# V of the dilated groups evicted at full height and reordered by SBUF transfers, with a new beginning and end of the program

## The chip, the cores and the metric

The kernel runs on one core of a Trainium2 chip. The metric is the device time of one execution in microseconds (us); lower is better. Engines are named as in the profile: PE is TensorE (PEld its weight loads), DVE is VectorE, ACT is ScalarE, POOL is GpSimd, SP is SyncE, which here only issues transfers. SPq, ACTq and so on are the instruction queues of the engines.

## The reference

A decoder trunk of two layers on 512 tokens of 1024 numbers, all fp32. Each layer adds half of a SwiGLU network, then a mixer, then half of a second SwiGLU network; a last norm follows.

```python
for l in range(DEPTH):                       # DEPTH = 2
    x = x + 0.5 * swiglu(rms_norm(x, norm_ffn1[l]), ...)
    x = x + hybrid_mixer(rms_norm(x, norm_mix[l]), ...)
    x = x + 0.5 * swiglu(rms_norm(x, norm_ffn2[l]), ...)
return rms_norm(x, norm_final)

def swiglu(x, w_gate, w_up, w_down):
    return (jax.nn.silu(x @ w_gate) * (x @ w_up)) @ w_down
```

The mixer projects its input once to queries, keys and values of 16 heads of 64 and to two gates. Twelve heads are dilated window attention in three groups of four, with dilations 1, 4 and 16 and partial rotary embedding of queries and keys; a query of a group with dilation d reads the tokens t, t-d, t-2d and so on. The groups are merged by their softmax denominators. Four heads are stick-breaking attention: instead of a softmax, a weight is the product of a sigmoid and of all later (1 - sigmoid), which is computed as an exponential of a running sum. The two results are projected, gated, added and projected again.

## The kernel before

**Layout and products.** Activations lie transposed: eight tiles `x0` to `x7` of 128 features by 512 tokens. A product in fp32 is made of three matmuls (`mm3`, lines 141 to 144): activation and weight are each split into a high and a low part in a rounded format, and hi x hi, lo x hi, hi x lo are added in one PSUM bank. `project` (line 146) does so over the eight feature tiles; so a 128 x 512 result costs 24 matmuls. PSUM has eight banks in four pairs with the tags m, t, o and s.

**Weights.** The class `Weights` (lines 45 to 94) streams all weights once, in order of use. SP issues transfers of 512 KB (`wraw`); ACT casts each quarter of 128x512 to its high part (`whi`, line 76) and DVE subtracts it for the low part (`wlo`, line 77), two quarters ahead of their use. A quarter serves four 128x128 blocks, twelve matmuls of 128x512.

**Norm.** `Norm` (lines 157 to 237): `scale` splits x times the gain into `xh` (ACT, line 179) and `xl` (DVE, line 180); `square` sums the squares; `finish` makes the row factor as `rt` (a column per token tile) and, through a matmul against the identity into a PSUM bank `pb`, as `rb` (a copy by ACT, line 236).

**Beginning.** ACT loads its function table, SP issues the gain, x0, the first two weight quarters and the other x tiles, and then the rest of the weights. The first pair of FFN tiles runs the gate projection `pg` to its end, then the up projection `pu`. ACT alone casts the weights.

**Mixer.** First come the values. With tokens as rows, four token tiles of 512 columns are made twice: half 0 holds the values of group 1 and the stick-breaking heads, half 1 those of the groups with dilation 4 and 16. `split_v` (lines 357 to 361) evicts PSUM to SBUF as a high part (ACT, line 359) and a low part (DVE, line 360). Half 0 is evicted in 8 pieces of 128x256 (tiles `v0`, `vs`). Half 1 goes to one tile `v12` in which the rows are ordered by the residue of the token modulo 4; since the engines write other partitions than they read only in blocks of 32, this takes 16 pieces of 32 rows by 512 columns.

Then `qk_pair` (lines 384 to 417) makes the queries and keys of a pair of heads: with rotary embedding, DVE multiplies (line 393) and shuffles (394), POOL multiplies and adds (395, 396), ACT casts (409 for queries, 413 for keys), DVE subtracts (410, 415), and SP copies the high parts of keys from one half of the partitions to the other (414). `stick` (lines 447 to 483) makes the stick-breaking weights of a head in four tiles of 128 to 512 columns: scores on PE (421, 422, 456), three ACT passes (460 to 462), DVE (463), a running sum on DVE (464), a subtraction on DVE (466), an exponential on ACT (467), which leaves `sw` in one of eight buffers with the tag "pp"; then PE transposes (476) and multiplies with the values (480). The dilated heads have scores, a softmax, transposes and the product with `v12` (620). Gates are further projections, evicted by DVE (493), put between these steps so that PE has work.

**What sets the order.** Each engine executes its own queue in order. Which instruction stands where in it is set by a scheduler that simulates the program when it is built and moves instructions within the limits of dependences and buffers; the order of the source is only its starting point. What it decides for one stretch can change with any edit inside it.

**End.** `finale` (lines 277 to 296) does the last two feature tiles in two halves of 256 tokens: DVE adds to x (288), the norm is finished, and eight products of x and `rb` (line 295; DVE for six of them, POOL for the two of `k == 2`) are written out by four transfers on SP (296).

## Time and profile before

| | |
|---|---|
| median of 3 runs | 2169.5 us (2168.34 to 2170.79) |
| profiled execution, time | 2166.81 us |
| its span in the trace | 2165.0 us |
| PE busy | 2136.6 us, 99% |
| DVE busy | 1209.4 us, 56% |
| ACT busy | 892.7 us, 41% |
| POOL busy | 374.4 us, 17% |
| data moved by transfers | 212.80 MB, mean 98 GB/s |

Busy times are unions of the instructions' spans on one engine; PE's instructions overlap in its pipeline, so their single durations are longer than the distance from one to the next. The trace is of one execution, and all times in the sections below are microseconds from the start of its span. The first mixer's values are made from about 380 to 434 us, its stick-breaking heads from 434 us on; the second layer repeats this about 1071 us later.

### The profile page before, as it was taken

To read this page: it belongs to the slowest core of one execution; us is meant where nothing else is said; L and a number is where in the kernel's file an instruction comes from. 1 tells how busy PE (TensorE), PEld (TensorE's weight loads), DVE (VectorE), ACT (ScalarE), POOL (GpSimd) and SP (SyncE) were. 2 spreads that over 40 slices of the span, in tenths; PEclk is the share of its full clock that TensorE was granted. 3 is DMA by queue.
4 is the path that set the end of the run, shared out by engine and by line. 5 is a ranking of instruction groups with operands and counts; after the bars stand their busy time and mean duration, and the time that the engine had idled before them with its cause. 6 is when DMAs were issued, how large, how long until landed. Compare 5 with 4: busy or idle time off the path is not lost.

```text
span 2165.0 us, 25866 instructions
## 1 busy us (share of the span) xinstructions
PE 2136.6 (99%) x9772; PEld 1764.2 (81%) x9772; DVE 1209.4 (56%) x1896; ACT 892.7 (41%) x1572; POOL 374.4 (17%) x396
## 2 busy tenths in 40 slices
PE   8999999999999999999999999999999999999998
PEld 7888888878887888888888888888788788888887
DVE  7544433589867655443354444336897666444433
ACT  5333323566564433332333333236664544333332
POOL 2222100021412122210022220000223212222100
PEclk9999999999999999999999999999999999999999
DMA  4333333232224233323233333333222233323222
GB/s 153 97 97 98 102 105 125 88 93 87 79 74 129 96 97 98 97 97 98 88 98 97 98 98 107 108 117 94 87 83 78 79 126 98 98 97 97 97 90 86
DMA packets 64621, 212.80 MB, mean 98 GB/s; under 512 B 7408, under 2 KB 9456, under 8 KB 64496
## 3 DMA queue, kind: packets, MB, share of 16 engines
q1 hardware_dynamic: 63920, 210.10, 30.4%
q8 instruction: 76, 1.25, 0.2%
q10 hardware_dynamic: 576, 1.05, 0.2%
q14 instruction: 49, 0.40, 0.1%
HBM read 200.63 MB, written 6.29 MB: 96 GB/s over the span
## 4 chain that ended last, share of the span: by engine, by line
PE 91%; DVE 5%; issue 2%; ACT 1%; POOL 1%; DMA 0%; SPq 0%; DVEq 0%; POOLq 0%; ACTq 0%
PE ps_o L142 14%; PE ps_o L143 14%; PE ps_o L144 14%; PE ps_m L142 9%; PE ps_m L143 9%; PE ps_m L144 9%; PE ps_t L143 5%; PE ps_t L142 5%; PE ps_t L144 5%; DVE wlo L77 1%; DVE sc L464 1%; PE ps_o L620 0%; POOL bn L554 0%; ACT pt L545 0%; PE ps_s L422 0%
## 5 line engine op out<-in xcount | busy, mean ns | idle before, releaser
L77 DVE TENSOR_TENSOR wlo<-wraw,whi 128x512 fp32r<-128x512 f32 x736 | 593.6, 809 | 584.1 <-ACT whi L76 583.5
L76 ACT CAST whi<-wraw 128x512 fp32r<-128x512 f32 x736 | 454.8, 621 | 963.0 <-PE ps_o L143 486.3
L142 PE MATMUL ps_m<-xh,whi 128*128 128x512 f32 x992 | 390.8, 394 | 8.7 <-ACT whi L76 6.1
L143 PE MATMUL ps_m<-xl,whi 128*128 128x512 f32 x992 | 391.3, 394 | 0.0
L144 PE MATMUL ps_m<-xh,wlo 128*128 128x512 f32 x992 | 390.4, 394 | 0.5 <-DVE wlo L77 0.5
L142 PE MATMUL ps_o<-fh,whi 128*128 128x512 f32 (+1 forms) x748 | 285.9, 382 | 0.0
L143 PE MATMUL ps_o<-fl,whi 128*128 128x512 f32 (+1 forms) x748 | 285.8, 382 | 0.0
L144 PE MATMUL ps_o<-fh,wlo 128*128 128x512 f32 (+1 forms) x748 | 285.8, 382 | 0.0
L260 POOL TENSOR_TENSOR fg<-fg,fs 128x512 f32<-128x512 f32 x88 | 116.4, 1325 | 867.0 <-ACT fs L259 867.0
L142 PEld LDWEIGHTS ps_m<-xh,whi 128*128 128x128 f32 x992 | 187.6, 189 | 49.2 <-ACT whi L76 7.0
L144 PEld LDWEIGHTS ps_m<-xh,wlo 128*128 128x128 f32 x992 | 187.6, 189 | 39.4 <-DVE wlo L77 2.0
L143 PEld LDWEIGHTS ps_m<-xl,whi 128*128 128x128 f32 x992 | 187.7, 189 | 37.9 <-DVE xl L180 0.8
L144 PE MATMUL ps_t<-xh,wlo 128*128 128x512 f32 x480 | 187.0, 390 | 0.0
L142 PE MATMUL ps_t<-xh,whi 128*128 128x512 f32 x480 | 187.0, 390 | 0.0
L143 PE MATMUL ps_t<-xl,whi 128*128 128x512 f32 x480 | 187.0, 390 | 0.0
L143 PE MATMUL ps_o<-xl,whi 128*128 128x512 f32 x448 | 174.5, 390 | 0.0
L142 PE MATMUL ps_o<-xh,whi 128*128 128x512 f32 x448 | 174.5, 390 | 0.0
L144 PE MATMUL ps_o<-xh,wlo 128*128 128x512 f32 x448 | 174.5, 390 | 0.0
L142 PEld LDWEIGHTS ps_o<-fh,whi 128*128 128x128 f32 x748 | 140.6, 188 | 30.1
L143 PEld LDWEIGHTS ps_o<-fl,whi 128*128 128x128 f32 x748 | 140.6, 188 | 30.0
L144 PEld LDWEIGHTS ps_o<-fh,wlo 128*128 128x128 f32 x748 | 140.6, 188 | 30.0
L261 POOL TENSOR_TENSOR fg<-fg,rb 128x512 f32<-128x512 f32 x88 | 116.3, 1324 | 6.3
(218 smaller groups left out, 2706.6 us busy)
## 6 DMA issues: line engine op xcount, KB each, us to landing
wraw<-in_w_dram SPq DMA_DIRECT2D x367, 512.0 KB, 3.5
spill<-x SPq DMA_DIRECT2D x16, 256.0 KB, 2.1
kh<-kh SPq DMA_DIRECT2D x32, 128.0 KB, 2.7
x<-spill SPq DMA_DIRECT2D x16, 256.0 KB, 3.5
x<-in_x_dram SPq DMA_DIRECT2D x8, 256.0 KB, 4.7
out_dram<-o SPq DMA_DIRECT2D x8, 256.0 KB, 2.2
wraw<-in_w_dram SPq DMA_DIRECT2D x2, 256.0 KB, 3.5
cr<-in_rope_dram ACTq DMA_DIRECT2D x2, 256.0 KB, 2.8
```

The source lines that it names most:

```text
L76: nc.scalar.copy(hi, src)
L77: nc.vector.tensor_sub(lo, src, hi.bitcast(F32))
L142: nc.tensor.matmul(ps, w[0], v[0], start=start, stop=False, skip_group_check=True)
L143: nc.tensor.matmul(ps, w[0], v[1], start=False, stop=False, skip_group_check=True)
L144: nc.tensor.matmul(ps, w[1], v[0], start=False, stop=stop, skip_group_check=True)
L260: nc.gpsimd.tensor_mul(g, g, s)
L261: nc.gpsimd.tensor_mul(g, g, norm.rb)
L464: nc.vector.tensor_tensor_scan(cv[:, ::-1], av[:, ::-1], ones[:, 0:1].to_broadcast([P, w]), 0.0, ALU.add, ALU.mult)
```

## The change

There are three parts, in one diff.

1. *Values.* Half 0 is evicted in 4 pieces of 128x512 into one tile per token tile (`v0s`). Half 1 is evicted in 8 pieces of 128x256 into tiles `vn`, which take the eight "pp" buffers that the `sw` tiles use later. Then 32 transfers of 32 rows by 512 words (64 KB) per mixer, issued by POOL, put the rows into `v12`.
2. *Beginning.* x0 is the first transfer of SP, the weights come in parts of 256 KB between the x tiles, the gain is issued by ACT. DVE casts the first weight quarter. Seven matmuls on a tile of zeros run into an unused bank. The first FFN pair runs over k with `pg` and `pu` side by side, for which the host packs the first 16 weight blocks in that order, and the squares are moved behind the last cast of x.
3. *End.* DVE's products read the norm factor from PSUM (`pb`) instead of its copy; POOL's two go on reading the copy `rb`.

```diff
@@ -31,6 +31,7 @@
+WARM = 7
@@ -54,17 +55,26 @@
         self.ready = {}
         self.done = 0
         self.chunk = None
+        self.early = []
+
+    def load(self, eng):
+
+        c, part = divmod(len(self.early), CB // QB)
+        if part == 0:
+            self.chunk = self.raw.tile([P, CB * P], F32, name="wraw", tag="wraw")
+        o = part * QB * P
+        eng.dma_start(self.chunk[:, o:o + QB * P], self.w[c, :, o:o + QB * P])
+        self.early.append(self.chunk)
 
     def fill(self, q):
         nc = self.nc
         while self.done <= q and self.done < self.nq:
             c, part = divmod(self.done, CB // QB)
-            if part == 0:
+            if self.done < len(self.early):
+                self.chunk = self.early[self.done]
+            elif part == 0:
                 self.chunk = self.raw.tile([P, CB * P], F32, name="wraw", tag="wraw")
-                step = P if c == 0 else CB * P
-                for o in range(0, CB * P, step * QB):
-                    e = min(o + step * QB, CB * P)
-                    nc.sync.dma_start(self.chunk[:, o:e], self.w[c, :, o:e])
+                nc.sync.dma_start(self.chunk, self.w[c])
             src = self.chunk[:, part * QB * P:(part + 1) * QB * P]
             i = self.done - (self.nq - HELD)
             if i < 0:
@@ -73,7 +83,10 @@
             else:
                 hi = self.hold.tile([P, QB * P], F32R, name="whi", tag=f"xh{i}")
                 lo = self.hold.tile([P, QB * P], F32R, name="wlo", tag=f"xl{i}")
-            nc.scalar.copy(hi, src)
+            if self.done:
+                nc.scalar.copy(hi, src)
+            else:
+                nc.vector.tensor_copy(hi, src)
             nc.vector.tensor_sub(lo, src, hi.bitcast(F32))
             self.ready[self.done] = (hi, lo)
             self.done += 1
@@ -121,17 +134,22 @@
     def bank(tag):
         return psum.tile([P, 512], F32, name="ps_" + tag, tag=tag)
 
+    weights = Weights(nc, rawp, splitp, hpool, win)
+    gain = const.tile([P, gains.shape[1]], F32, name="gain")
+    warm = hpool.tile([P, T], F32R, name="warm", tag=f"xh{KD - 1}")
+    nc.vector.memset(warm.bitcast(F32), 0.0)
+    nc.scalar.dma_start(gain, gains)
     nc.scalar.preload_act_table_set(SIGM)
-    gain = const.tile([P, gains.shape[1]], F32, name="gain")
-    nc.sync.dma_start(gain, gains)
-    weights = Weights(nc, rawp, splitp, hpool, win)
     xs = []
     for k in range(KD):
         t = xpool.tile([P, T], F32, name=f"x{k}", tag=f"x{k}")
         nc.sync.dma_start(t, xin[k])
         xs.append(t)
-        if k == 0:
-            weights.fill(0)
+        if k % 2 == 0:
+            weights.load(nc.sync)
+    ps = bank("o")
+    for i in range(WARM):
+        nc.tensor.matmul(ps, warm[:, 0:P], warm, start=True, stop=True, skip_group_check=True)
 
     ident = const.tile([P, P], F32, name="ident")
     make_identity(nc, ident)
@@ -176,7 +194,7 @@
             if not self.last:
                 hi = hpool.tile([P, T], F32R, name=f"xh{k}", tag=f"xh{k}")
                 lo = hpool.tile([P, T], F32R, name=f"xl{k}", tag=f"xl{k}")
-                nc.scalar.activation(hi, x, AF.Copy, bias=0.0, scale=gk)
+                self.cast = nc.scalar.activation(hi, x, AF.Copy, bias=0.0, scale=gk)
                 nc.vector.scalar_tensor_tensor(lo, x, gk, hi.bitcast(F32), ALU.mult, ALU.subtract)
                 self.h[k] = (hi, lo)
 
@@ -234,7 +252,7 @@
                                  start=True, stop=True, skip_group_check=True)
             rb = npool.tile([P, T], F32, name="rb", tag="rb", bufs=2)
             nc.scalar.copy(rb[:, :n * P], pb[:, :n * P])
-            self.rt, self.rb = rt, rb
+            self.rt, self.rb, self.pb = rt, rb, pb
 
     def ffn(norm, nxt, first):
         with ExitStack() as st:
@@ -246,12 +264,20 @@
             hs = []
             for f in range(NF):
                 pg, pu = [bank(b) for b in ("mt", "mt", "oo")[f % 3]]
-                project(pg, norm.h)
-                project(pu, norm.h)
-                if f == 0:
-                    if first:
+                if first and f == 0:
+
+                    for k in range(KD):
+                        if k + 4 < KD:
+                            norm.scale(k + 4)
+                        for ps in (pg, pu):
+                            mm3(ps, weights.block(), norm.h[k], k == 0, k == KD - 1)
+                    with tc.issue_after(norm.cast.ins):
                         for k in range(KD):
                             norm.square(k)
+                else:
+                    project(pg, norm.h)
+                    project(pu, norm.h)
+                if f == 0:
                     norm.finish_wide(nw, onesr)
                 g = wk.tile([P, T], F32, name="fg", tag="fg")
                 s = wk.tile([P, T], F32, name="fs", tag="fs")
@@ -290,9 +316,9 @@
             nxt.finish(c0 // P, (c0 + HT) // P)
             for k in range(0, KD, 2):
                 o = op.tile([P, 2, HT], F32, name="o", tag="o")
-                eng = nc.gpsimd if k == 2 else nc.vector
+                eng, r = (nc.gpsimd, nxt.rb) if k == 2 else (nc.vector, nxt.pb)
                 for i in range(2):
-                    eng.tensor_mul(o[:, i], xs[k + i][:, c], nxt.rb[:, :HT])
+                    eng.tensor_mul(o[:, i], xs[k + i][:, c], r[:, :HT])
                 nc.sync.dma_start(out[k:k + 2, :, c].rearrange("k p t -> p k t"), o)
 
     def mixer(norm, nxt):
@@ -363,17 +389,19 @@
             if half == 0:
                 v0, vs = [], []
                 for j in range(NT):
-                    sc = norm.rt[:, j:j + 1]
-                    for lst, nm, off in ((v0, "v0", 0), (vs, "vs", 256)):
-                        t = vp.tile([P, 4, 2, HD], F32R, name=f"{nm}_{j}", tag=f"{nm}_{j}")
-                        split_v(t, pv[0][j][:, off:off + 256], sc)
-                        lst.append(t)
+                    t = vp.tile([P, 8, 2, HD], F32R, name=f"v0s_{j}", tag=f"v0s_{j}")
+                    split_v(t, pv[0][j], norm.rt[:, j:j + 1])
+                    v0.append(t[:, 0:4])
+                    vs.append(t[:, 4:8])
             else:
                 v12 = vp.tile([P, 4, 8, 2, HD], F32R, name="v12", tag="v12")
                 for j in range(NT):
-                    for r in range(4):
-                        src = slice(32 * r, 32 * r + 32)
-                        split_v(v12[32 * j:32 * j + 32, r], pv[1][j][src], norm.rt[src, j:j + 1])
+                    for g in range(2):
+                        t = pp.tile([P, 4, 2, HD], F32R, name="vn", tag="pp")
+                        split_v(t, pv[1][j][:, 256 * g:256 * g + 256], norm.rt[:, j:j + 1])
+                        for r in range(4):
+                            nc.gpsimd.dma_start(v12[32 * j:32 * j + 32, r, 4 * g:4 * g + 4].bitcast(F32),
+                                              t[32 * r:32 * r + 32].bitcast(F32))
 
         def to_t(ap):
             return ap.rearrange("p (j m r) -> p j r m", j=NT, m=32, r=4)
@@ -689,10 +717,10 @@
         outer.close()
 
     norm = Norm(0, SIGM)
-    for k in range(KD):
+    for k in range(4):
+        if k % 2 == 0:
+            weights.fill(k // 2)
         norm.scale(k)
-        if k == 3:
-            weights.fill(1)
     mask = const.tile([P, 640], F32, name="mask")
     nc.sync.dma_start(mask, masks)
     mnat, mperm, msb = mask[:, 0:256], mask[:, 256:512], mask[:, 512:640]
@@ -758,10 +786,12 @@
 
     import numpy as np
 
-    def ffn(g, u, dn):
+    def ffn(g, u, dn, first=False):
         g = a[g][l].reshape(KD, P, NF, P).transpose(2, 0, 1, 3)
         u = a[u][l].reshape(KD, P, NF, P).transpose(2, 0, 1, 3)
         gu = np.stack([g, u], 1).reshape(-1, P, P)
+        if l == 0 and first:
+            gu[:2 * KD] = gu[:2 * KD].reshape(2, KD, P, P).transpose(1, 0, 2, 3).reshape(-1, P, P).copy()
         dn = a[dn][l].reshape(NF, P, KD, P).transpose(2, 0, 1, 3).reshape(-1, P, P)
         return [gu, dn]
 
@@ -798,7 +828,7 @@
-    return ffn("ffn1_w_gate", "ffn1_w_up", "ffn1_w_down") + mix + ffn("ffn2_w_gate", "ffn2_w_up", "ffn2_w_down")
+    return ffn("ffn1_w_gate", "ffn1_w_up", "ffn1_w_down", True) + mix + ffn("ffn2_w_gate", "ffn2_w_up", "ffn2_w_down")
```

Some line numbers move: in the new file ACT's weight cast is line 87, the rotary lines on POOL are 423 and 424, the casts of queries and keys 437 and 441, the stick-breaking lines on ACT 488 to 490 and 495.

PE at the very beginning of the program, before; `ps_m` is the gate product, `xh` and `xl` are the parts of x0, x1 and so on.

```order
L142 MATMUL ps_m<-xh_111,whi 128x512
L143 MATMUL ps_m<-xl_112,whi 128x512
L144 MATMUL ps_m<-xh_111,wlo 128x512
L142 MATMUL ps_m<-xh_115,whi 128x512
L143 MATMUL ps_m<-xl_116,whi 128x512
L144 MATMUL ps_m<-xh_115,wlo 128x512
```

The same place after; `ps_t` is the up product.

```order
L152 MATMUL ps_o<-warm 128x512 x7
L160 MATMUL ps_m<-xh_124,whi 128x512
L160 MATMUL ps_t<-xh_124,whi 128x512
L161 MATMUL ps_m<-xl_125,whi 128x512
L161 MATMUL ps_t<-xl_125,whi 128x512
L162 MATMUL ps_m<-xh_124,wlo 128x512
L162 MATMUL ps_t<-xh_124,wlo 128x512
L160 MATMUL ps_m<-xh_128,whi 128x512
L160 MATMUL ps_t<-xh_128,whi 128x512
L161 MATMUL ps_m<-xl_129,whi 128x512
L162 MATMUL ps_m<-xh_128,wlo 128x512
L161 MATMUL ps_t<-xl_129,whi 128x512
```

The two products now alternate k by k behind seven matmuls on zeros.

POOL from the setting up of the mixer on, before (`cr` and `sr` are the rotary tables, `qa` and `qb` the halves of the rotary sum).

```order
L323 MEMSET kl 64x512 x4
L354 TENSOR_TENSOR cr<-cr,rb 128x512
L355 TENSOR_TENSOR sr<-sr,rb 128x512
L395 TENSOR_TENSOR qb<-qb,sr 128x512
L396 TENSOR_TENSOR qa<-qa,qb 128x512
```

The same place after.

```order
L349 MEMSET kl 64x512 x4
L380 TENSOR_TENSOR cr<-cr,rb 128x512
L381 TENSOR_TENSOR sr<-sr,rb 128x512
L403 DMA v_3190<-vn 32x512 x32
L423 TENSOR_TENSOR qb<-qb,sr 128x512
L424 TENSOR_TENSOR qa<-qa,qb 128x512
```

All 32 transfers stand ahead of the first rotary product of the mixer.

ACT in the first head of the stick-breaking part, before; `sw` of 128x384 and 128x512 are the third and fourth score tile of that head, `qh` are the queries of the next pair.

```order
L462 ACTIVATE sw<-sw 128x384
L409 CAST qh<-qa 64x512 x2
L460 ACTIVATE sw<-ps_s 128x512
L461 ACTIVATE sw<-sw 128x512
L76 CAST whi<-wraw 128x512
L462 ACTIVATE sw<-sw 128x512
L467 ACTIVATE sw<-sc 128x3x32x4
L76 CAST whi<-wraw 128x512
L460 ACTIVATE sw<-ps_s 128x128
L467 ACTIVATE sw<-sc 128x4x32x4
```

The same place after; line 495 is the exponential that was line 467.

```order
L488 ACTIVATE sw<-ps_s 128x384
L489 ACTIVATE sw<-sw 128x384
L488 ACTIVATE sw<-ps_s 128x512
L490 ACTIVATE sw<-sw 128x384
L489 ACTIVATE sw<-sw 128x512
L490 ACTIVATE sw<-sw 128x512
L87 CAST whi<-wraw 128x512
L495 ACTIVATE sw<-sc 128x3x32x4
L87 CAST whi<-wraw 128x512
L495 ACTIVATE sw<-sc 128x4x32x4
L437 CAST qh<-qa 64x512 x2
```

The query casts stood between the passes over the third and the fourth tile, and stand behind the fourth tile's exponential now.

## Rows read from the trace of the kernel before

**Rows 1.** The page, parts 1 and 4: busy time; shares of the chain.

```profile
PE 2136.6 (99%) x9772; PEld 1764.2 (81%) x9772; DVE 1209.4 (56%) x1896; ACT 892.7 (41%) x1572; POOL 374.4 (17%) x396
...
PE 91%; DVE 5%; issue 2%; ACT 1%; POOL 1%; DMA 0%; SPq 0%; DVEq 0%; POOLq 0%; ACTq 0%
```

**Rows 2.** The view of TensorE's waits, whole span: us in total, times, longest.

```profile
PE ps_s L421 <- DVE sc L466: 3.0, 3, 1.3
...
PE ps_m L142 <- DVE gate L493: 2.5, 2, 1.2
PE ps_s L421 <- issue: 1.5, 2, 1.0
PE ps_o L620 <- DVE ptl L431: 1.4, 2, 0.7
...
PE ps_t L476 <- ACT sw L467: 0.5, 2, 0.3
```

**Rows 3.** Timeline near 463: start, us, engine, line, [idle before <- releaser].

```profile
463.64 0.36 PE L421 MATMUL ps_s<-kh,qh 128*128 128x256 f32 x1 [1.31 <-DVE sc L466]
```

**Rows 4.** The chain that ended last, near 451 to 463: start, us, what.

```profile
451.71 1.63 POOL qa L396
453.37 0.63 ACT qh L409
...
460.54 2.24 DVE sc L464
462.81 0.70 DVE sc L466
```

**Rows 5.** By windows: PE, PEld, DVE, ACT, POOL busy (x count); clock; DMA; GB/s.

```profile
0.00:14.39 14.39, 8.47 (x24) 5.82 (x25) 9.04 (x15) 10.91 (x18) 1.60 (x9) 1.00 0.79 280
417.00:441.00 24.00, 24.00 (x109) 19.70 (x108) 22.87 (x32) 18.94 (x29) 0.00 (x0) 1.00 0.26 80
461.00:469.00 8.00, 6.43 (x23) 4.75 (x22) 7.53 (x10) 3.15 (x7) 3.58 (x3) 0.79 0.23 74
```

**Rows 6.** The source view of line 360: durations in ns, least, median, largest.

```profile
L360 DVE SCALAR_TENSOR_TENSOR v<-ps_s,rt,v x16: 737/744/757, 416.4 to 1500.4; 32x512 fp32r<-32x512 f32 x16
...
L360 DVE SCALAR_TENSOR_TENSOR v<-ps_m,rt,v x4: 476/480/485, 394.5 to 1466.2; 128x256 fp32r<-128x256 f32 x4
```

**Rows 7.** The source view of line 414, transfers inside SBUF on SP.

```profile
L414 SPq DMA_DIRECT2D kh<-kh x32: 461/467/1403, 434.9 to 1667.7; - x32
...
DMA to landing us min/median/max: 2.2/2.7/4.4
```

**Rows 8.** Timeline of the beginning, columns as in group 3.

```profile
0.74 0.39 SPq L126 DMA_DIRECT2D gain<-in_g_dram  x1
...
1.19 0.42 SPq L131 DMA_DIRECT2D x<-in_x_dram  x1
...
1.66 0.90 SPq L67 DMA_DIRECT2D wraw<-in_w_dram  x2
...
3.99 0.72 ACT L179 ACTIVATE xh<-x,gain 128x512 fp32r<-128x512 f32 x1 [1.97 <-DMA x<-in_x_dram]
...
5.14 0.60 ACT L76 CAST whi<-wraw 128x512 fp32r<-128x512 f32 x1
...
5.79 0.80 PE L142 MATMUL ps_m<-xh,whi 128*128 128x512 f32 x1 [5.79 <-ACT whi L76]
...
9.37 0.63 PE L142 MATMUL ps_m<-xh,whi 128*128 128x512 f32 x1
...
9.80 0.63 PE L143 MATMUL ps_m<-xl,whi 128*128 128x512 f32 x1
```

**Rows 9.** Timeline of the end, columns as in group 3.

```profile
2154.41 0.42 DVE L288 SCALAR_TENSOR_TENSOR x<-ps_o,x 128x256 f32<-128x256 f32 x1 [4.07 <-PE ps_o L144]
...
2158.08 0.37 ACT L236 COPY rb<-ps_s 128x256 f32<-128x256 f32 x1 [1.70 <-PE ps_s L233]
2158.48 3.15 DVE L295 TENSOR_TENSOR o<-x,rb 128x256 f32<-128x256 f32 x6 [1.32 <-ACT rb L236]
```

## The prediction

> **What bounds the kernel now.** I read the page's shares first, then who TensorE waits for, then the places of the long waits, and last the engines around them. TensorE is busy 2136.6 of 2165.0 us and holds 91% of the chain that ended last [rows 1]. So work taken off VectorE or ScalarE is worth nothing by itself: the change can win only where TensorE stands still, about 28 us, plus what it loses at a lower clock. The waits of TensorE show which places these are [rows 2]: scores that wait for `sc` of line 466 (3.0 us in three waits), transposes that wait for `sw` of line 467 (0.5), a score matmul released by "issue" (1.5 in two), a projection that waits for a `gate` (2.5 in two), values that wait for `ptl` (1.4 in two). All of them lie in the two mixers, 0.5 to 1.5 us each. The rest is the beginning and the end of the program.
>
> The largest ends at 463.64, after 1.31 us for DVE line 466 [rows 3]. Its cause is in the chain [rows 4]: POOL adds the rope halves until 453.34, only then ACT casts `qh` at 453.37, and the four ACT passes and the VectorE scan of the *previous* head's last score tile stand behind that cast in ACT's order, so that the scan starts at 460.54 (2.24) and line 466 at 462.81. The wait costs more than itself: in 461 to 469 the granted clock is 0.79 on the mean [rows 5]. Between the levels 2.4 and 1.2 GHz that is (1 - 0.79) / 0.5 x 8 = 3.4 us at the lower one, hence 1.7 us of work lost.
>
> **V, eviction.** Removed per mixer: 16 casts and 16 subtractions of 32x512; VectorE's take 0.744 each [rows 6], 11.9 us. Added: 8 of 128x256 at 0.48, 3.8 us. Half 0 goes from 8 of 0.48 to 4 of 128x512; ACT and VectorE save another microsecond or so there. So some 8 to 9 us of VectorE go per layer, and ACT's casts of the same pieces become half as many. This lies in a stretch where VectorE is busy 22.87 of 24.00 us, but TensorE is busy all 24.00 of it [rows 5]. Priced by itself it is 0: the projections, 109 matmuls in a row, cover it. It pays only by what VectorE then does earlier.
>
> **The order behind V.** The scheduler writes the whole attention stretch of both layers anew. What matters is ACT: before, the `qh` casts stand between the third and fourth score tile of a head; after, they stand behind the head's fourth exponential (the order fences above). The wait for POOL [rows 4] then no longer delays that head. By that I count the waits for `sc` and `sw` as gone, 3.0 + 0.5, and with them the 1.7 us at the lower clock: 5.2. The waits for "issue" and `gate` (1.5 + 2.5) have the same VectorE queue behind them, which now runs earlier, but the order does not remove their cause: I count half, 2.0. The `ptl` waits (1.4) lie at the dilated values, ahead of which more projections stand now: half, 0.7. Together 7.9 for both layers. Bounds: 0, if as many new waits come, and about 11, if everything named goes.
>
> **V, the transfers.** POOL has no DMA in the trace of before. After, 32 transfers of 64 KB stand per mixer in POOL's queue between the products for `cr`, `sr` and the first rope addition. What does one cost POOL? From below: an SBUF to SBUF transfer of twice the size costs SP 0.467 us to issue; from above: it lands after 2.7 us [rows 7]. Landing is not occupancy of a queue; transfers of one queue land beside each other, so I stay near the lower row but take about double, 1.0, since here POOL is to do the work. A gain of the queue is excluded: it was empty. The first can start when the first piece is evicted, near 416.9 (the first old piece starts at 416.4 on VectorE [rows 6]); 32 x 1.0 ends near 449. The rope addition must be done when ACT reaches the `qh` casts; laying the new order on the old durations I get 455.2, so two POOL passes of 1.6 [rows 4] must begin by 452.0: 35.1 / 32 = 1.10 per transfer. The next user of that cast has about 2.4 us of slack (estimate from the same layout), which makes the point from which TensorE pays **1.17 per transfer**. At 1.0 the cost is 0, and the cover is the projections and first scores. Without that cover: every further 0.1 costs 2 x 32 x 0.1 = 6.4 us. The score tiles `sw` share eight buffers with the new pieces; the first needs only four transfers done, the eighth all 32, and by the same layout that is some 50 us after V began: hidden at 1.0. The transfers move 2 MB per mixer on engines that are at 0.26 share [rows 5]: no bound.
>
> A rule that speaks against this: VectorE is busy 95% of the time just where POOL issues [rows 5]. The Trainium skill, "SBUF — State Buffer" ("A bandwidth-pool intuition that's wrong"), gives a transfer issued by GpSimd as 620 ns alone and 3100 ns beside a VectorE tensor copy, since GpSimd can't write the descriptors meanwhile; by 3100 the sum would be 2 x 32 x (3.1 - 1.17) = 124 us slower. Its section "Who interferes with whom" spares operations with two inputs or an input in PSUM, and those are what the stretch holds; by that rule and 620 the sum stays. No row here shows either.
>
> **The beginning.** Before: `x` is issued at 1.19 behind the gain, its cast starts at 3.99, the weight cast at 5.14, the first matmul at 5.79, and successive matmuls at 9.37 and 9.80 are still 0.43 apart [rows 8], which is the lower level (the clock column of the window says 1.00 there; the spacing decides). The first 24 matmuls end at 14.39; at 0.22 each (24.00 us / 109) they would take 5.3, so the beginning costs 9.1 us [rows 5]. After: `x` goes first on SP (0.74 against 1.19), the weights are issued right behind it, so land near 4.0 to 4.7 (2.8 us from issue to use for `x`; at most 3.5 for the weights). VectorE casts them (0.6), first matmul near 5.0. Then VectorE has `xl` and `wlo` (about 0.7 each) on the path, so k = 0 runs to about 7.3, from where TensorE is fed: one k asks 6 matmuls of it, 1.3 us. What it loses is then 7.3 - 1.3 = 6.0 instead of 9.1: **3.0 saved**. The seven dummy matmuls cost nothing, since TensorE is idle until 5; I count that they bring the clock up by the end of k = 0. Bounds: 3.7 if the weights land early, and 1.3 if the clock stays low some 4 us more, or if loading binds: one k needs 384 KB, at 280 GB/s [rows 5] 1.4 us, just about TensorE's pace.
>
> **The end.** The copy of line 236 (0.37 and a hand-over) leaves VectorE's path, about 0.4. Six products from PSUM instead of SBUF: 3.15 / 6 = 0.53 each against 0.42 for an operation of this size that reads PSUM [rows 9], 0.65 saved. But POOL's two products still wait for the copy, and the last transfers go out after VectorE's last product: **0.9**, bounds 0.4 and 1.05.
>
> **Sum.** 3.0 + 0.9 + 7.9 = 11.8 us. The profiled execution took 2166.8 (span 2165.0 and 1.8 around it), so 2155.0; the median of the timed runs, 2169.5, lies 2.7 above it: **2157.7**, say 2158.
>
> **Rivals.** *(1) Waits only move.* TensorE waits in the attention stretch for whichever engine is late, and the new order puts others late: a later `qh` cast makes the second head of a pair wait. For it: three waits for `sc` in two layers with the same instructions [rows 2], so small shifts of time decide where they fall. Against it: the cause of the largest is out of ACT's way. Then beginning and end alone, 3.9 us: 2165.6. *(2) POOL's queue is late, and it is slower.* Place: the first rope addition behind the 32 transfers; ACT's `qh` cast waits for it, and behind that cast in ACT's order are the weight casts, without which TensorE has nothing. Point: 1.17 per transfer; all gains are used up at 1.17 + 11.8 / 64 = 1.35. At the middle of the bounds, 1.58, it costs 26 us: 2184. One way to it from rows: if a transfer has to wait out the VectorE operation in progress (22.87 / 32 = 0.71), it costs 0.467 + 0.71 = 1.18, and two such waits 1.9, 47 us more: 2205. At the upper bound, 2.7, 98 us: 2256. For it: VectorE hardly rests there; against it: the issue row of 0.467. *(3) More than forecast.* All named waits go, 11 + 3.7 + 1.05, with the clock loss near the dilated values too: about 2150 or less.
>
> **Chances.** Forecast 0.53 (2150 to 2163); only moved 0.18 (2163 to 2172); POOL late 0.16 (2174 to 2256, mostly below 2205); more than forecast 0.13. Within 0.2% (4.3 us, about what a measurement of this kernel can tell from no change) is 2165.2 to 2173.8: 0.16, nearly all of the second case, whose rest lies just below. Faster 0.53 + 0.13 + 0.02 = 0.68; slower 0.16. Range 2148 to 2172: it holds the first two cases and the upper half of the last, leaving out the late queue.
>
> **What would show it.** POOL's row of 32 issues: below 1.17 us each and the rope addition starting as VectorE's shuffle ends, not as a transfer does; else rival 2. In the waits of TensorE: `sc` and `sw` below 1 us in total, no 0.79 stretch near 461; a new name with over 3 us is rival 1. First matmul near 5.0, and the 48 matmuls of the first pair done at 17 us instead of 20. Six products of VectorE at 0.42 each at the end, starting without the copy. The forecast is wrong if POOL's issues cost well over a microsecond, or if the matmuls that wait are those of the second head.

## The result, and the profile after

The changed kernel takes **2152.47 us** (median of 6 runs, 2151.74 to 2153.1); the kernel before took 2169.35 in the 6 runs beside it. The ratio is 0.9924, 95% interval 0.9914 to 0.9935: 16.9 us, or 0.8%, faster. The forecast was 2158 (2148 to 2172). The two profiled executions differ by less, 2166.81 against 2152.92 and spans of 2165.0 against 2151.1, since the profiled execution of before was one of its fastest; below I go by stages of several traces.

First the page of the changed kernel, parts 1, 4 and 6 (busy time; shares of the chain; the new transfers with KB each and median us to landing), to be read beside [rows 1].

```profile
PE 2131.8 (99%) x9779; PEld 1760.5 (82%) x9779; DVE 1181.5 (55%) x1874; ACT 876.9 (41%) x1547; POOL 402.0 (19%) x460
...
PE 91%; DVE 3%; ACT 2%; issue 2%; POOL 1%; DMA 1%; DVEq 0%; SPq 0%; POOLq 0%; ACTq 0%
...
v<-vn POOLq DMA_DIRECT2D x64, 64.0 KB, 4.1
```

TensorE is busy 4.8 us less though it computes the same and the seven matmuls on zeros besides, which fits matmuls that last longer at the lower clock. Of VectorE's 28 us less, 18 are the evictions, some 9 us per mixer; POOL's 28 us more are the issues of the new transfers.

TensorE's waits after (us in total, times, longest), to be read beside [rows 2]:

```profile
PE ps_t L160 <- ACT od1h L471: 2.6, 2, 1.3
PE ps_o L152 <- DVE ones L157: 1.5, 1, 1.5
...
PE ps_s L449 <- DVE sc L494: 1.2, 2, 0.6
PE ps_m L160 <- DVE qb L422: 1.0, 2, 0.5
...
PE ps_s L449 <- DMA kh<-kh: 0.8, 1, 0.8
PE ps_o L630 <- DVE ptl L459: 0.7, 2, 0.3
```

The five waits of [rows 2] made 8.9 us. What is left of them is `sc` 1.2 and `ptl` 0.7; `sw`, "issue" and `gate` are gone. New are a shuffle `qb` (1.0) and one key copy (0.8); together 3.7, so 5.2 less. The wait for `od1h`, which stood in the kernel before too, is unchanged, and the wait for `ones` lies ahead of the dummy matmuls and costs nothing.

By windows after (columns as in [rows 5]): the beginning up to the end of the first FFN pair's 48 matmuls, V's eviction with the transfers, the stretch of [rows 5] that had the lower clock (458 to 466 here, since the changed kernel is 3 us ahead), and the end.

```profile
0.00:16.76 16.76, 15.13 (x56) 11.73 (x57) 11.08 (x18) 11.52 (x17) 1.43 (x9) 1.00 0.78 272
414.00:438.00 24.00, 23.22 (x106) 19.08 (x105) 15.60 (x26) 14.01 (x27) 15.84 (x32) 1.00 0.74 186
...
458.00:466.00 8.00, 7.62 (x37) 6.09 (x35) 7.90 (x14) 2.20 (x5) 3.25 (x3) 1.00 0.24 66
...
2138.00:2151.00 13.00, 3.01 (x24) 2.67 (x22) 3.31 (x12) 1.50 (x4) 1.41 (x2) 0.70 0.24 83
```

VectorE is busy 15.60 of 24.00 us where it was busy 22.87, and the granted clock is 1.00 where it was 0.79. Read in windows of 5 us, the first trace of before has three in the mixers that are well below 1, the one of [rows 5] (0.66 from 465) and two more:

```profile
585.00:590.00 5.00, 5.00 (x22) 4.48 (x22) 4.80 (x6) 3.15 (x6) 1.64 (x2) 0.69 0.31 105
1720.00:1725.00 5.00, 4.52 (x12) 3.25 (x13) 3.12 (x4) 1.60 (x3) 1.87 (x2) 0.66 0.00 0
```

They took 0.34 x 5.00 + 0.31 x 5.00 + 0.34 x 4.52 = 4.8 us of work. The second trace of before has two (0.66 from 465, 0.68 from 480), both in mixer 1; after has none until the end at 2140.

By stages, from the start of VectorE's additions that close a stage, in us (a mixer's stage holds the next network's first products too):

| trace | to the end of the first network | mixer 1 | mixer 2 | the end, from the sixth tile's last addition |
|---|---|---|---|---|
| before | 372.27 | 600.25 | 601.39 | 43.25 |
| before, once more | 372.81 | 601.98 | 600.28 | 43.29 |
| after | 369.43 | 595.23 | 594.26 | 44.34 |
| difference, first trace | -2.84 | -5.02 | -7.13 | +1.09 |

So the mixers gave 12.2 us by these two traces (12.8 against the second one of before), the beginning 2.8, and the end **lost** 1.1. Of the 12.2, 5.2 are TensorE's shorter waits and 4.8 the stretches at the lower clock; I have not placed the remaining 2.2.

### The profile page after: what moved, and what is told of

The parts are those of the page before. It is cut to its first block, busy times and chain, and to the rows that moved or that the text cites. A ratio compares the mean times of both kernels' runs of the same rounds, so it can differ in the third digit from the quotient of the medians.

```text
span 2151.1 us, 26016 instructions
## 1 busy us (share of the span) xinstructions
PE 2131.8 (99%) x9779; PEld 1760.5 (82%) x9779; DVE 1181.5 (55%) x1874; ACT 876.9 (41%) x1547; POOL 402.0 (19%) x460
## 3 DMA queue, kind: packets, MB, share of 16 engines
q10 hardware_dynamic: 720, 1.08, 0.2%
## 4 chain that ended last, share of the span: by engine, by line
PE 91%; DVE 3%; ACT 2%; issue 2%; POOL 1%; DMA 1%; DVEq 0%; SPq 0%; POOLq 0%; ACTq 0%
PE ps_o L160 14%; PE ps_o L161 14%; PE ps_o L162 14%; PE ps_m L160 9%; PE ps_m L161 9%; PE ps_m L162 9%; PE ps_t L160 5%; PE ps_t L161 5%; PE ps_t L162 5%; DVE wlo L90 1%; ACT gate L684 1%; PE ps_s L450 0%; PE ps_s L449 0%; POOL qb L423 0%; POOL qa L424 0%
## 5 line engine op out<-in xcount | busy, mean ns | idle before, releaser
L90 DVE TENSOR_TENSOR wlo<-wraw,whi 128x512 fp32r<-128x512 f32 x736 | 586.5, 799 | 585.4 <-ACT whi L87 584.5
```

The source lines that it names most:

```text
L90: nc.vector.tensor_sub(lo, src, hi.bitcast(F32))
```

## The experiments

**Which part gives what.** Three kernels with one part each, and the kernel before once more for a second trace. The edits are pieces of the diff above: its piece on `v0s` and `vn` alone; its pieces on `Weights`, the start, `ffn` and the packing alone; its pieces on `pb` alone.

> The values part alone (half 0 in 128x512 pieces, half 1 in 128x256 pieces and 32 transfers on POOL), beginning and end as in the kernel before. Theory: the two traces differ by 2.84 us when the first mixer starts, by 7.86 when it ends and by 14.99 at the last norm, so the values part alone is worth 5.0 + 7.1 = 12.2 us in the two mixers: about 2157 against 2169.4. Rival: the mixers' gain hangs on where in time the new beginning puts them, and the part alone is worth only the waits for sc and sw, 3.5 to 5 us: 2164 to 2166.

Measured: 2157.17 us (2156.77 to 2158.17), ratio 0.9947 (0.9935 to 0.9959), 11.7 us faster. Mixers of 594.54 and 594.52 us.

> The new beginning alone; mixers and end as in the kernel before. Theory: 2.8 us less, all of it before the first FFN tile is done (48 matmuls end near 16.8 us), 2166.5. Rival: the shift of 2.8 us moves waits of the mixers too, and the sum is 5 us or more, or nothing.

Measured: 2165.67 us, ratio 0.9986 (0.9977 to 0.9995), 3.2 us faster; 369.59 us to the end of the first network, mixers of 601.91 and 600.31 as in the kernel before.

> DVE's products at the end read PSUM, all else as before. Theory: the six last products take 0.35 us each instead of 0.53, but still begin behind ACT's copy; the last transfer is issued 1.0 us earlier and the time falls by 0 to 1.1 us, 2168.3 to 2169.4. My prediction had counted 0.4 for the copy besides: the products would begin 0.4 us earlier after the matmul than before. Rival: the transfers, issued closer together, land later by as much, and nothing is gained.

Measured: 2168.78 us, ratio 1.0000 (0.9991 to 1.0009): nothing.

> The kernel before once more, for a second trace. If the 16.9 us between the medians against 13.9 between the two profiled executions is scatter of single executions, its span lies 1 to 4 us above the 2165.0 of the first trace, and the additional time stands in the mixers (a longer stretch at the lower clock) or in the last transfers. If it is the profiled execution that differs in kind, the span is 2165.0 again.

Measured: span 2166.2, 1.2 above the first. Mixer 1 alone was 1.7 longer, mixer 2 1.1 shorter. Mixer 1 took 601.88 and 601.91 in the traces of the kernels with the end alone and the beginning alone too, so the first trace of before was short by 1.7 there. That is scatter of single executions, as supposed. The second trace has no stretch at the lower clock in mixer 2, which fits its 1.1; in mixer 1 both traces have two, and what makes the 1.7 I did not follow up. The parts add up: 11.7 + 3.2 + 0.1 = 15.0 of 16.9, within the intervals.

**The order or VectorE's time?** The values part changes two things at once: VectorE and ScalarE have less to do, and the scheduler, seeing that, writes another order. The first kernel keeps the new order and gives back a part of the work, VectorE's and ScalarE's together:

```diff
 split_v(t, pv[1][j][:, 256 * g:256 * g + 256], norm.rt[:, j:j + 1])
+split_v(t, pv[1][j][:, 256 * g:256 * g + 256], norm.rt[:, j:j + 1])
```

> The values part alone, but each of the eight full-height evictions of half 1 is done twice by ACT and by DVE: 3.8 us of DVE's time and as much of ACT's come back per mixer, of some 9 that the change frees, while the order of the attention stretch stays that of the values part (32 of 9746 places on PE differ, none on POOL and SP). Theory 1, the new order is what pays: 2157.2 as the values part alone, within 1.5. Theory 2, the time freed on VectorE pays: 3.8 of 9.2 of the 11.7 us are lost again, about 2162.

Measured: 2162.67 us (2158.83 to 2163.47), ratio 0.9970 (0.9959 to 0.9981): 5.5 of the 11.7 us lost again. Mixers of 598.27 and 595.51, 3.7 and 1.0 longer than with the values part alone. Its waits of TensorE:

```profile
PE ps_m L142 <- DVE qb L397: 2.7, 2, 1.3
```

and two windows of mixer 1:

```profile
470.00:480.00 10.00, 8.23 (x37) 6.42 (x38) 8.07 (x15) 8.98 (x19) 1.51 (x2) 0.92 0.29 79
480.00:490.00 10.00, 10.00 (x45) 8.34 (x44) 6.56 (x12) 4.67 (x10) 2.92 (x1) 0.91 0.34 105
```

The wait for VectorE's shuffle has grown from 1.0 to 2.7, and behind it the clock has fallen: 0.08 x 8.23 + 0.09 x 10.00 = 1.6 us of work lost. These two are 3.3 of the 4.7 us that the mixers lost. A second stretch at the lower clock takes another 1.6 us of mixer 1 (0.91 in 645 to 650, 0.75 in 650 to 655, both 1.00 with the values part alone); it follows the wait for `od1h`, which is 2.6 in both kernels, so whether the time given back brings it or chance, this trace does not show. (0.96 us of the 5.5 lie ahead of the mixer, where single executions scatter.) So the order alone does not hold the gain; the freed time does its part. TensorE's grown wait is for VectorE, but the run does not part VectorE from ScalarE.

The second kernel is the kernel before with its own evictions, and only the cast held back that my prediction named as the cause (`exps[0, 3]` is the fourth exponential of the first head):

```diff
-nc.scalar.copy(view_q(hi[own]), src)
+if kind == "rope" and ropes[0] < 2:
+    ropes[0] += 1
+    with tc.issue_after(exps[0, 3].ins):
+        nc.scalar.copy(view_q(hi[own]), src)
+else:
+    nc.scalar.copy(view_q(hi[own]), src)
```

> The kernel before with its evictions, and one thing: the first query casts behind the rope (line 409) are held until the fourth exponential of the first stick-breaking head has been issued on ACT, as in the changed kernel. The scheduler orders the rest of the stretch anew around that. My prediction's step: the waits for sc and sw near 463 and in the second layer go, with the stretch at the lower clock, 3.5 to 5.2 us: 2163.7 to 2165.4. Theory 2, the cast's place is not what matters, VectorE's load is: no change, 2168.9, or other waits of the same size.

Measured: 2174.99 us (2169.82 to 2178.73), ratio 1.0027 (1.0017 to 1.0036): slower. Its waits of TensorE:

```profile
PE ps_s L427 <- DVE sc L472: 4.5, 4, 2.1
PE ps_o L626 <- DVE ptl L437: 3.5, 5, 1.6
...
PE ps_m L142 <- DVE qb L395: 2.6, 4, 0.8
```

The waits for `sc` are longer than before (4.5 against 3.0), and so are those for `ptl` (3.5 against 1.4); `qb` has joined. With the cast held, TensorE waits elsewhere, while VectorE has as much to do. The scheduler also changed 1206 places on TensorE for this edit, so it shows that the cast's place is not enough, not what it is worth by itself.

**Where POOL's limit is.** Every transfer issued twice:

```diff
-for r in range(4):
+for r in [0, 1, 2, 3] * 2:
     nc.gpsimd.dma_start(v12[32 * j:32 * j + 32, r, 4 * g:4 * g + 4].bitcast(F32),
                       t[32 * r:32 * r + 32].bitcast(F32))
```

> The values part alone with every transfer of POOL issued twice, 64 per mixer. An issue was measured at 0.50 us, so POOL's queue is busy 32 us instead of 16, plus what it waits for pieces and landed transfers: by the limit of my prediction, 32 x 1.17 = 37.4 us, still just in time, 2157 to 2160. If the limit is nearer, every microsecond beyond it costs 2 us: 2165 and more, with the first rope product waiting behind a transfer.

Measured: 2206.62 us, ratio 1.0172 (1.0159 to 1.0185), 49 us above the values part alone. (The scheduler counts the added transfers and writes yet another order, close to 1400 of 9772 places on PE, so that the 49 us belong to both.) In the changed kernel POOL's rows are (the source view of the 64 issues in ns, then the timeline with the last transfer of mixer 1 and the first rope product):

```profile
L403 POOL DMA_DIRECT2D v<-vn x64: 496/496/659, 414.2 to 1499.7; - x64
...
435.90 0.50 POOL L403 DMA_DIRECT2D v<-vn  x1 [0.41 <-DMA v<-vn]
445.34 1.58 POOL L423 TENSOR_TENSOR qb<-qb,sr 128x512 f32<-128x512 f32 x1 [8.94 <-DVE qb L422]
```

The queue is done at 436.4 and POOL rests 8.94 us until VectorE's shuffle: the transfers are hidden. With the values part alone the same rope product starts at 448.14, since the old beginning is some 4 us longer. With twice as many transfers (timeline of POOL, then the chain that ended last):

```profile
455.91 1.31 POOL L397 TENSOR_TENSOR qb<-qb,sr 128x512 f32<-128x512 f32 x1
457.15 1.52 POOL L377 DMA_DIRECT2D v<-vn  x3
```

```profile
450.25 4.38 DMA v<-vn
454.63 0.64 ACT sw L462
```

The rope product starts at 455.91 as the queue lets it, and at 454.63 ACT's first pass over a score tile (line 462 there) starts when a transfer has landed, since it needs a buffer of a `vn` piece. So the transfers hold up two engines at once. The next kernel takes one hold-up away: the pieces lie in the tiles of x, which are empty in the mixer.

```diff
-t = pp.tile([P, 4, 2, HD], F32R, name="vn", tag="pp")
+t = xpool.tile([P, 4, 2, HD], F32R, name="vn", tag=f"x{2 * j + g}")
```

> The values part with every transfer issued twice, as in the run before, but the eight pieces lie in the buffers of the x tiles, which stand empty in the mixer, so that the score tiles sw no longer wait for transfers. The chain of the run with doubled transfers leads from a transfer's landing to ACT's first pass over a score tile. Theory: that buffer is the limit, and with it gone most of the 49 us go: 2157 to 2172; what is left is the rope product behind the queue. Rival, the limit of my prediction: POOL's queue delays the rope product, and the time stays near 2200.

Measured: 2198.39 us, ratio 1.0139 (1.0126 to 1.0152). The buffers were worth 8 of the 49 us (437 places on PE differ between the two); the time stays near 2200, as the rival said. POOL (timeline), two windows of mixer 1, and the largest of TensorE's waits:

```profile
454.62 1.30 POOL L397 TENSOR_TENSOR qb<-qb,sr 128x512 f32<-128x512 f32 x1
455.87 2.49 POOL L377 DMA_DIRECT2D v<-vn  x5
```

```profile
460.00:480.00 20.00, 14.36 (x54) 10.60 (x54) 15.16 (x30) 16.05 (x36) 0.00 (x0) 0.66 0.11 34
480.00:500.00 20.00, 15.30 (x60) 11.47 (x61) 17.44 (x30) 15.68 (x31) 4.24 (x4) 0.83 0.06 13
```

```profile
PE ps_s L423 <- DVE sc L468: 13.4, 8, 4.2
```

The queue is still in the rope product's way, which starts at 454.62 against 448.14 with the values part alone. And the price is not one for one: TensorE idles 5.64 and 4.70 us in the two windows, 10.3 together (1.2 with the values part alone), and its clock is 0.66 and 0.83 there, which takes 0.34 x 14.36 + 0.17 x 15.30 = 7.5 us more. The two are most of the 19.0 that mixer 1 lost (613.54 against 594.54). But what TensorE waits for is mainly `sc`, 13.4 us against 1.2 with the values part alone, and its order differs from that kernel's in over 1200 places. How much of the loss is the late queue itself, and how much the order that the scheduler wrote for it, is not shown.

**Another queue.** `nc.gpsimd` of the transfers replaced by `nc.sync`:

> The values part alone with the 32 transfers issued by SP instead of POOL, where the weight loads stand. Theory: POOL's queue cost nothing in the mixer, but its closing drain takes 5.3 us longer in a program in which POOL issues transfers, and ends 1.06 us after SP's last; with SP that 1.06 us goes, 2156.1 plus or minus what SP's order does. Rival: 32 issues of about 0.47 us, each waiting for its piece, hold up the weight loads behind them: TensorE waits for weights near 420 us and the time is 2160 or more.

Measured: 2176.73 us, ratio 1.0036 (1.0024 to 1.0048). The largest waits of TensorE, and SP in mixer 1:

```profile
PE ps_s L423 <- DMA kh<-kh: 11.2, 2, 5.7
PE ps_m L142 <- ACT whi L76: 10.1, 5, 5.8
```

```profile
417.80 20.47 SPq L377 DMA_DIRECT2D v<-vn  x32
438.37 1.16 SPq L416 DMA_DIRECT2D kh<-kh  x2
439.59 15.17 SPq L67 DMA_DIRECT2D wraw<-in_w_dram  x5
```

SP is taken for 20.47 us by the 32 transfers. The weight loads and key copies behind them are late: 11.2 us for key copies, and 10.1 instead of 5.9 for casts of weights. The rival holds, though here too the order differs from that of the values part. In these two kernels POOL's queue is the better place, with nothing urgent behind the transfers.

**Beginning and end of the changed kernel.** Without the seven dummy matmuls, and their tile:

```diff
-for i in range(WARM):
-    nc.tensor.matmul(ps, warm[:, 0:P], warm, start=True, stop=True, skip_group_check=True)
```

> The changed kernel without the seven matmuls on zeros and their tile. In the changed kernel the spacing of matmuls falls from 0.43 to 0.23 near 6.5 us, in the kernel before near 11. Theory: without them the matmuls from 5 to some 10.5 us run at the lower level, and about half of 4 us is lost: 2154 to 2154.8. Rival: the casts and transfers of the beginning set the pace there, and the dummies are worth nothing: 2152.5.

Measured: 2155.60 us (2154.82 to 2156.36), 3.1 above the changed kernel; the first network ends at 372.36 instead of 369.43. Timeline of TensorE with the dummies, then without:

```profile
1.46 3.35 PE L152 MATMUL ps_o<-warm 128*128 128x512 f32 x7 [1.46 <-DVE ones L157]
4.98 0.77 PE L160 MATMUL ps_m<-xh,whi 128*128 128x512 f32 x1 [0.17 <-DVE whi L89]
...
6.40 0.44 PE L161 MATMUL ps_t<-xl,whi 128*128 128x512 f32 x1
6.68 0.39 PE L162 MATMUL ps_m<-xh,wlo 128*128 128x512 f32 x1
6.91 0.40 PE L162 MATMUL ps_t<-xh,wlo 128*128 128x512 f32 x1
```

```profile
4.90 0.77 PE L155 MATMUL ps_m<-xh,whi 128*128 128x512 f32 x1 [4.90 <-DVE whi L89]
...
9.73 0.45 PE L157 MATMUL ps_t<-xh,wlo 128*128 128x512 f32 x1
10.02 0.40 PE L155 MATMUL ps_m<-xh,whi 128*128 128x512 f32 x1
10.25 0.39 PE L155 MATMUL ps_t<-xh,whi 128*128 128x512 f32 x1
```

With them the spacing falls from 0.43 to 0.23 at 6.5, 1.5 us after the first product; without them at 9.8, 4.9 us after it. 3.3 us more at half speed would be 1.7; from the twelfth product on the kernel is 1.5 behind (9.73 against 8.28) and stays so to the end of the pair. The rest of the 2.9 is one wait that the changed kernel does not have and the expectation did not count:

```profile
PE ps_m L155 <- DVE fg L279: 1.5, 1, 1.5
```

TensorE stands until 42.16 for a PSUM bank that `fg` has to read out, and `fg` needs the norm's factor, which VectorE starts to write at 40.60 instead of 37.63. Why the factor comes that much later I did not follow up.

All eight products of the end on VectorE, and no copy:

```diff
-eng, r = (nc.gpsimd, nxt.rb) if k == 2 else (nc.vector, nxt.pb)
 for i in range(2):
-    eng.tensor_mul(o[:, i], xs[k + i][:, c], r[:, :HT])
+    nc.vector.tensor_mul(o[:, i], xs[k + i][:, c], nxt.pb[:, :HT])
```

> The changed kernel with all products of the end on DVE, from PSUM, and no copy by ACT there. Theory: the end is set by POOL's closing drain, which ends 5.3 us after POOL's last product; with no product there it is long done, DVE begins 0.4 us earlier and SP's last transfer decides: 1.0 to 1.5 us less, 2151.2 against 2152.5. Rival: eight products in a row on DVE (8 x 0.35) issue the last transfer as late as before, no change.

Measured: 2151.21 us, ratio 0.9921 (0.9908 to 0.9933). The end takes 42.68 us instead of 44.34 (same places as in the table). The products of the changed kernel's end and of this one's (timeline, columns as in [rows 9]):

```profile
2143.09 0.37 ACT L254 COPY rb<-ps_s 128x256 f32<-128x256 f32 x1 [1.71 <-PE ps_s L251]
2143.49 2.07 DVE L321 TENSOR_TENSOR o<-x,ps_s 128x256 f32<-128x256 f32 x6 [1.32 <-ACT rb L254]
2143.59 1.41 POOL L321 TENSOR_TENSOR o<-x,rb 128x256 f32<-128x256 f32 x2 [11.21 <-ACT rb L254]
```

```profile
2142.57 2.73 DVE L322 TENSOR_TENSOR o<-x,ps_s 128x256 f32<-128x256 f32 x8 [0.94 <-PE ps_s L251]
```

The last instructions of both, by source line: duration in ns (least, median, largest), and start of the first and last.

```profile
L863 POOLq DRAIN  x3: 34/102/6717, 2143.6 to 2150.8; - x3
L863 SPq DRAIN  x3: 7/7/7, 2149.2 to 2150.6; - x3
```

```profile
L864 POOLq DRAIN  x3: 34/102/6649, 2011.2 to 2148.7; - x3
```

A drain is an instruction at the end of each engine's queue. In the changed kernel POOL's row of it lasts 6.717 us, from 2143.6 to 2150.3, and closes the program 1.1 us after SP, whose drains begin at 2149.2. The row starts while POOL's last products still run (1.41 us), so 5.3 us are the drain itself. With the new end it begins at 2011.2 and is long over. In the kernel before, the row lasts 1.827 us, of which 1.77 are the products.

Both ideas together, the end on VectorE and the pieces in the tiles of x:

> The changed kernel with both: all products of the end on DVE, and the eight pieces in the buffers of the x tiles. The order on PE is the changed kernel's. Theory: at one transfer each the buffers cost at most the 0.8 us that one score tile waited for a transfer, so 0 to 1 us besides the 1.0 to 1.5 of the end: 2150.2 to 2151.5. Rival: the buffers were no limit at one transfer each, and it equals the kernel with the new end alone.

Measured: **2150.30 us** (2149.47 to 2150.8), ratio 0.9916 (0.9903 to 0.9929), the fastest of all, 2.2 below the changed kernel. Mixers of 594.18 and 594.14, the same as with the new end alone (594.25 and 594.13), so at one transfer each the buffers cost nothing; what it gains is the end (42.07). The 0.9 us between this kernel and the one with the new end alone lie where the two are alike (in the traces 0.6 in the first network and 0.6 in the end), so I do not count them.

## Why the prediction was right, and where it was not

The sign, the size and the range held: 11.8 us forecast, 16.9 measured by the medians (13.9 and 15.1 us by the two traces of before against that of after). In part that is luck: the mixers gave 4.3 us more than I had counted and the end 2.0 less. Term by term, in the order of its sum:

- **The beginning, 3.0: right**, 2.84 in the traces, 3.2 alone. First product at 4.98 instead of 5.79 [rows 8] (forecast 5.0), the 48 by 17. The dummies, to which I had given no share of their own, carry nearly all of it: without them 3.1 us are lost again, about half by the clock and half by the wait for `fg`.
- **V's eviction, 0 by itself: the step that failed.** I had said that TensorE is busy through that stretch [rows 5], so that work saved there is worth nothing, and laid the gain on one cast's place in ACT's order [rows 4]. Holding that cast made the kernel 5.4 us slower, in an order that differs in other places too, and giving back 3.8 us per mixer of VectorE's work, and as much of ACT's, in the new order cost 5.5 us. The pieces cost 0.477 each as expected [rows 6]. VectorE works off a queue through the whole attention stretch; that an eviction which ends 9 us earlier is time that it has some 50 us later is shown for one wait, that for `qb` near 478 (1.0 to 2.7 when the time is given back), and is argued for the rest. I had written "it pays only by what VectorE then does earlier" and then counted nothing for it. How the gain divides between the order and the freed time stays open: giving back 3.8 of some 9 us took 4.7 of the 12 back in the mixers, of which 1.6 are the second stretch at the lower clock.
- **The mixers, 7.9: mis-sized**, 12.2 in the two traces, 11.7 by the values part alone. The term that was too small is the clock: I had counted one stretch at the lower level, 1.7 us, where the first trace of before had three (4.8 us) and the second two. The waits came out a little below my count, 5.2 against 6.2: `issue` and `gate`, which I had halved, are gone entirely, but 1.2 of `sc` stayed and 1.8 are new. The third rival named the clock; the result lay between it and the forecast.
- **The transfers, 0 at 1.0 us each: right, for a smaller price.** One issue takes 0.496 us, next to the lower row of [rows 7] and not the double; besides, POOL waited 5.4 us in all for landed transfers. The rule of the Trainium skill ("SBUF — State Buffer", "Who interferes with whom") held: beside VectorE's operations with two inputs the issues were not held up (0.659 us at the longest, with VectorE busy 15.60 of 24.00 us), and nothing like 3100 ns was seen. **The limit, 1.17 us per old transfer, was too generous in what lies beyond it**: 64 transfers per mixer, by issue time as much as 32 of 1.0 each, cost 41 to 49 us where I expected none. The rope product was late, as I had said; two things were missing: that POOL waits for landed transfers before it issues more (12.2 and 13.7 us for 128 transfers, without and with the buffers of x), and that ten microseconds of stall cost another seven or eight by the clock. The new orders have a part in those 41 to 49 us that no run separates.
- **The end, 0.9: wrong**, -1.1 in the trace, 0 alone. The products did get faster (2.07 for six against 3.15 [rows 9]), but for another reason than the one I gave: I had read the mean of 0.53 as the price of an operand in SBUF, and only the two products that ran beside POOL's were slow (see the last section). They still began 0.40 us after the copy's start, exactly as before, because the program puts the two readers of that PSUM bank one behind the other (their row names ACT's copy as what released them); without the copy they begin 0.79 us after the matmul instead of 1.17. And I had not seen that POOL's closing drain, not SP's last transfer, would end the program once POOL issues transfers.
- **Only moved (rival 1)** happened on a small scale: `qb` and a key copy, 1.8 us. **POOL late (rival 2)** did not happen with 32 transfers.

## What to carry to other kernels

When the busiest engine waits for a second one in short stalls, the second one's time can be worth something even where it is hidden at that moment: follow its queue to the next stall before pricing a saving at zero. A stall costs more than itself where the clock falls behind it, so count the windows below full clock among the gain. Before giving a rarely used engine's queue a chain of transfers, look for what stands behind them, how many can be in flight, and what that queue does when the program ends.

## What the runs showed of the hardware that was not expected

- POOL's drain at the end of the program grows with the transfers of 64 KB that POOL has issued. Its row is 1.83 us with none, 7.08 with 64 (values part alone) and 12.31 with 128; without the 1.77 us of POOL's own products at its start that is 0.06, 5.3 and 10.5, about 0.08 us per transfer. That these are over long before does not help; a POOL instruction late in the program delays it.
- A VectorE product of two SBUF operands beside a POOL product takes more than twice its time. In the kernel before, the two of VectorE's six last products that run beside POOL's two take 0.94 each; with one operand in PSUM, the same product beside POOL's takes 0.41 (timeline rows of single products, before and after):

```profile
2158.83 0.94 DVE L295 TENSOR_TENSOR o<-x,rb 128x256 f32<-128x256 f32 x1
2159.69 0.94 DVE L295 TENSOR_TENSOR o<-x,rb 128x256 f32<-128x256 f32 x1
```

```profile
2143.83 0.41 DVE L321 TENSOR_TENSOR o<-x,ps_s 128x256 f32<-128x256 f32 x1
```

  Before POOL's products and after them, products of two SBUF operands take 0.41 to 0.43 too, so an operand in SBUF costs nothing by itself there: two times 0.53 is nearly the whole of the 1.08 us that the products gained. POOL's own products fell from 0.90 to 0.73 each. The Trainium skill ("SBUF — State Buffer", "Who interferes with whom") describes this contention for two SBUF inputs against a POOL instruction that reads SBUF, and none with one SBUF input; both agree with these rows.
- 32 transfers of 64 KB raise the share of the transfer engines from 0.26 to 0.74 in their 24 us, at 186 GB/s instead of 80, and take 4.1 us each to land, more than the 2.7 of twice the size in [rows 7]. I had called these engines no bound.
